# A float32 decoder layer on one core: weight tiles split in one pass, rings of three, one more Strassen pair in each mixer unit

## The chip, the core and the metric

The kernel runs on one core of a Trainium2 chip. The metric is the device time of one execution in microseconds (us). Its engines work in parallel, each on its own queue in order: TensorE (PE) multiplies, VectorE (DVE) and ScalarE (ACT) work elementwise, GpSimd (POOL) and SyncE (SP) here mostly issue DMAs. PE writes to PSUM, which has eight banks of 512 float32 columns; everything else lies in SBUF.

## What is computed

One layer of a decoder over 256 rows of 4096 values. In the reference:

```python
u = rmsnorm(h, norm_w[l])
proj = u @ w_in[l]
a_q, a_f, a_i, a_g, b_q, b_k, b_v, b_g, gate_a, gate_b = jnp.split(proj, split_idx, axis=-1)
o_a = hgrn2_mix(a_q, a_f, a_i, lb_all[l]).astype(u.dtype)
o_a = rmsnorm(o_a, hgrn_norm_w[l]).reshape(bsz, seq, A_WIDTH) * jax.nn.silu(a_g)
...
o_b = diff_attention(qb, kb, vb, lam, slopes)
o_b = rmsnorm(o_b, subln_w[l], SUBLN_EPS) * (1.0 - lam_init)
o_b = o_b.reshape(bsz, seq, B_WIDTH) * jax.nn.silu(b_g)
y = (jax.nn.sigmoid(gate_a) * (o_a @ w_branch_a[l])
     + jax.nn.sigmoid(gate_b) * (o_b @ w_branch_b[l]))
h = h + y @ w_out[l]
return rmsnorm(h, final_w)
```

Nearly all of the work is the four matrix products with w_in (4096 by 24576), the two branch weights (2048 by 4096 each) and w_out (4096 by 4096), all float32.

## The kernel before

**Precision.** A product of float32 values is made of three matmuls in the faster fp32r type: the activations and the weights are each split into a high part (a rounded copy) and a low part (the rest), and high x high, high x low and low x high are added up in PSUM. The activations' parts are made once and stay in SBUF; the weights are streamed from HBM and split on the way: ACT copies the high part (L162), DVE subtracts to get the low part (L163).

**Units and pairs.** The work is a list of units of 1024 output columns: 16 mixer units (m0 to m15: four groups of the HGRN2 recurrence and four of attention, two units each), gate units 0 to 7, four times a branch-A and a branch-B unit, four output units. A unit runs over the contraction in pairs of 128-row tiles: 16 pairs, in a branch unit 8. Each pair's weights are one DMA of 1 MB into a raw tile of 2048 columns (four blocks of 512), of which there are three (`wraw`); SP issues the load when an earlier raw tile has been read out.

**Plain and Strassen pairs.** A plain pair ("P") is 2 tiles x 4 blocks (2 row tiles by 2 column halves) x 3 matmuls = 24 matmuls. A Strassen pair ("S") treats the 2 by 2 blocks of activations and weights in the Winograd variant of Strassen's scheme: 7 products instead of 8, so 21 matmuls, into seven banks. It needs sums of activation blocks, made once for a pair (`s_form`, L375 to L386, one `sf` tile), and sums of weight blocks, made for each raw tile on DVE: L143 adds two blocks in place, L144 makes a third sum in a tile `wt` of its own, L148 subtracts that from two blocks in place. At the end of a unit the seven banks are combined by DVE and ACT (`evict`, L304 to L321). Which pairs are S is listed: SPLIT (L438) for the mixer units from the fourth on and gate units 0 and 1, SPLIT_G (L439) for gate units 2 to 6, SPLIT_B (L468) for branch units, Y_SPLIT for the output units.

**The stream.** `Stream` cuts a pair's weights into chunks: two of 1024 columns for P, four for S (1024, 1024, 512 from `wt`, 1024). Chunks take turns in rings of tiles `hi` and `lo` (1024 columns): 5 of each up to the end of gate unit 0, 7 after it. A ring's tile is free again when PE has read it. `split_to` writes the splitting of a chunk into the program SPLIT_AHEAD (3, later 5) chunks before the matmuls that use it.

**Order.** A scheduler puts each engine's instructions in order when the program is built: of those that are ready in its own estimate, that of the highest priority. The splitting and the combining of banks get a higher priority (`high_priority`, L155 and L290); the matmuls of one bank stay in their order, those of different banks may change places.

**Work between.** The mixers' own steps (transposes, scores, softmax, the heads' norm and gating in `finish`, L690 to L727) are put into a queue and written out one or two after each pair (`step`); those that use PE go only beside pairs 14, 15, 0, 1 and 2, where the four banks of the Strassen products are unused.

Of the kernel before, what the change touches and what calls it, by code (L numbers as in the profile page):

```python
# [37 lines left out]
SPLIT_AHEAD = 3  # L38
# [5 lines left out]
def trunk_kernel(ctx, tc, xT, x, nw, w_mix, w_gate, w_branch, w_out, lbt, hnw, lamv, slw, fw, out):  # L44
# [48 lines left out]
    class Stream:  # L93
# [3 lines left out]

        def __init__(self):
            self.src = []
            self.kind = []  # L100
            self.chunks = []
            self.first = []
            self.raw = {}
            self.split = {}
            self.loaded = 0
            self.done = 0
            self.ring = [(whi, wlo)]
            self.at = 0
# [23 lines left out]
        def tiles(self):  # L132
            a, b = self.ring[self.at % len(self.ring)]
            self.at += 1
            hi = a.tile([P, HALF], F32R, name="hi", tag="hi")
            lo = b.tile([P, HALF], F32R, name="lo", tag="lo")
            return hi, lo

        def sums(self, i, c):
            w = self.raw[i]  # L140
            if c == 0:
                t = self.raw[i, "T"] = wt.tile([P, 512], F32, name="wt", tag="wt")
                dve.tensor_tensor(w[:, 0:512], w[:, 0:512], w[:, 512:1024], op=ALU.add)  # L143
                dve.tensor_tensor(t, w[:, 0:512], w[:, 1536:2048], op=ALU.subtract)  # L144
            if c == 2:
                t = self.raw[i, "T"]
                b = w[:, 512:1536].rearrange("p (a c) -> p a c", a=2)
                dve.tensor_tensor(b, b, t.unsqueeze(1).to_broadcast([P, 2, 512]), op=ALU.subtract)  # L148

        def split_to(self, n):  # L150
            while self.done < min(n, len(self.chunks)):
                i, c = self.chunks[self.done]
                self.load_to(i + 1)
                hi, lo = self.tiles()
                with tc.high_priority(AHEAD):  # L155
                    if self.kind[i] == "S":
                        self.sums(i, c)
                    t = self.raw[i, "T"] if c == 2 else self.raw[i][:, (0, 1024, 0, 512)[c] :]
                    w = 512 if c == 2 else HALF
                    m = HALF // 2 if i < HEAD // 2 else w  # L160
                    for k in range(0, w, m):
                        act.activation(hi[:, k : k + m], t[:, k : k + m], AF.Copy)  # L162
                        dve.tensor_tensor(lo[:, k : k + m], t[:, k : k + m], f32(hi[:, k : k + m]), op=ALU.subtract)  # L163
                if c == (3 if self.kind[i] == "S" else 1):
                    del self.raw[i]
                    self.raw.pop((i, "T"), None)
# [3 lines left out]
        def take(self, i):  # L170
            for n in range(self.first[i], self.first[i] + (4 if self.kind[i] == "S" else 2)):
# [91 lines left out]
    ORDER = (("p5", "P1"), (0, 1), ("P6",), ("P7", 2))  # L263
# [4 lines left out]
    def wide_unit(srcs, kinds, pf, sf, bank, final, post=None, tail=1, kt0=0, pre=None):  # L268
# [55 lines left out]
        def plain(n, c, hi, lo, blocks):  # L324
            kt = kt0 + 2 * n + c
            for t, m in blocks:
                o = 512 * (m if c else 1 - m)
# [3 lines left out]
        def fn(n, c, hi, lo):  # L331
            if pre and c == 0:
                pre(n)
            if kinds[n] == "S":
                for i, b in enumerate(ORDER[c]):
# [9 lines left out]
            if n <= last - tail:  # L345
                plain(n, c, hi, lo, [(t, m if c else 1 - m) for t in range(2) for m in range(2)])
                return
            held[n, c] = hi, lo
            if n < last or c == 0:
                return  # L350
            for blocks in ([[(t, 1 - m)] for t in range(2) for m in range(2)] if tail == 1
                           else [[(t, m) for m in range(2)] for t in range(2)]):
                for (k, c2), w in held.items():
                    plain(k, c2, *w, blocks)
# [83 lines left out]
    SPLIT = (4, 6, 8, 10, 12, 13)  # L438
    SPLIT_G = (0, 2, 4, 6, 8, 10, 12, 13, 14)  # L439
    us = {}  # L440
    s_pools = [sp] * 6
# [19 lines left out]
    def more_sums(n):  # L461
        if n == 0:
            s_pools[:] = [sp2] * 3
# [56 lines left out]
    def branch_unit(q):  # L520
# [46 lines left out]
        def post_b(n):  # L567
            if n == 0:
                g_load(1)
            if q == 3:  # L570
                if n == 0:
                    s_pools[:] = [sp] * 6 + [sp2]
# [102 lines left out]
    with tc.tile_pool(name="tmp", bufs=1) as tmp:  # L675
# [8 lines left out]
        def half(tag):  # L684
            return tmp.tile([P, HPG, P], F32, name=tag, tag=tag)

# [3 lines left out]
        def finish(T, seg, eps, scale, slot):  # L690

            n = 1024 // seg
            o, sq, g = T["o"], T["sq"], T["g"]

            def stats():
                ss = tmp.tile([P, n], F32, name="ss", tag="ss", bufs=2)
                dve.tensor_reduce(ss, fl(sq).rearrange("p (n c) -> p n c", c=seg), axis=AX.X, op=ALU.add)
                act.activation(ss, ss, AF.Sqrt, scale=1.0 / seg, bias=eps)
                dve.reciprocal(ss, ss)
                T["ss"] = ss  # L700

            def gate():
                sg = big("z")
# [4 lines left out]
            def apply():  # L708
                o3 = fl(o).rearrange("p (n c) -> p n c", c=seg)
                dve.tensor_tensor(o3, o3, T["ss"].unsqueeze(2).to_broadcast([P, n, seg]), op=ALU.mult)  # L710
                dve.tensor_tensor(fl(o), fl(o), fl(T["silu"]), op=ALU.mult)
# [65 lines left out]
        def hgrn_group(g):  # L777
# [43 lines left out]
            def s1d():  # L821
                km, kx, dec = T["z"], half("kx"), T["dec"]
                dve.tensor_tensor(km, km, T["sg"], op=ALU.mult)
                dve.tensor_tensor(kx, km[:, :, 0:P], dec[:, :, 1].to_broadcast([P, HPG, P]), op=ALU.mult)
                T["kx"] = kx

            def s2():
                qm, qx, dec = T["q"], half("qx"), T["dec"]
# [219 lines left out]
```

## Time and profile before

| | us |
|---|---|
| median of 3 runs | 2788.42 |
| lowest, highest | 2786.64, 2789.74 |
| the profiled execution | 2788.72 |
| its span, first to last instruction | 2786.9 |
| PE busy | 2760.9 |
| DVE busy | 2341.9 |
| ACT busy | 1616.8 |

By PE's weight matmuls the mixer units end at 1421 us, gate unit 1 ends at 1588, gate units 2 to 6 at 2006, the branch units at 2437. A row of a group names line, engine, operation, tiles (out<-in), shape and count, then busy time, the mean ns of one, and the idle time of the engine before them with what ended it. A row of the timeline has start and length in us first; instructions of one kind that follow each other are merged into one row with their count. PE's matmuls overlap: a matmul's length in the trace is more than the distance to the next.

### The profile page before, as it was taken

The numbers are of one execution on the slowest core, as the hardware profiler recorded it, in microseconds if no ns is written. First come the engines' busy times: TensorE is split into PE (matmuls) and PEld (weight loads), VectorE is DVE, ScalarE is ACT, GpSimd is POOL, SyncE is SP. The second block draws the span as 40 slices with busy tenths as digits, with TensorE's granted clock in tenths as the row PEclk, the third lists the DMA queues.
The fourth block names the chain that finished last, engine by engine and source line by source line (L and its number), as shares of the span: only waits on it lengthen the run. The fifth ranks groups of instructions, "written<-read, shape, count | busy, mean of one in ns | idle before, by whom it ended". The sixth has DMA issues, their size and how long they took to land.

```text
span 2786.9 us, 32847 instructions
## 1 busy us (share of the span) xinstructions
PE 2760.9 (99%) x12361; PEld 2274.4 (82%) x12361; DVE 2341.9 (84%) x2689; ACT 1616.8 (58%) x1937; POOL 74.6 (3%) x124
## 2 busy tenths in 40 slices
PE   9999999999999999999999999999999999999998
PEld 7888888888888888888888887778888888888886
DVE  6784888888888888888888899999877878989997
ACT  7664656656555555665556555555655554555554
POOL 0010000000000000000000000000000000010000
PEclk9999999999999999999999999999999999999999
DMA  9555455555555555555556555555675766766665
GB/s 343 188 181 203 180 185 202 198 199 193 188 191 210 190 192 187 198 206 189 191 196 245 201 212 211 222 214 201 241 263 218 250 218 227 259 235 237 248 255 214
DMA packets 96767, 597.76 MB, mean 214 GB/s; under 512 B 11856, under 2 KB 12128, under 8 KB 31200
## 3 DMA queue, kind: packets, MB, share of 16 engines
q1 hardware_dynamic: 88272, 566.29, 55.9%
q0 software_dynamic: 8336, 29.38, 2.8%
q8 instruction: 96, 1.57, 0.2%
q14 instruction: 63, 0.52, 0.1%
HBM read 571.51 MB, written 24.12 MB: 214 GB/s over the span
## 4 chain that ended last, share of the span: by engine, by line
PE 78%; DVE 14%; DMA 4%; issue 2%; ACT 2%; POOL 0%; DVEq 0%; ACTq 0%; POOLq 0%
PE ps_w L286 75%; DVE lo L163 9%; DVE w L148 2%; DMA w<-in_w_gate 1%; ACT hi L162 1%; DMA w<-in_w_out 1%; DVE w L143 1%; DVE wt L144 1%; PE ps_q L759 1%; DMA w<-in_w_mix 0%; DMA yl<-y_dram 0%; DVE ut L369 0%; PE ps_sc L842 0%; PE ps_o L857 0%; PE ps_t L718 0%
## 5 line engine op out<-in xcount | busy, mean ns | idle before, releaser
L162 ACT ACTIVATE hi<-w 128x1024 fp32r<-128x1024 f32 (+1 forms) x1203 | 1231.5, 1053 | 1009.8 <-PE ps_w L286 497.4
L163 DVE TENSOR_TENSOR lo<-w,hi 128x1024 fp32r<-128x1024 f32 (+1 forms) x1203 | 1436.9, 1219 | 309.0 <-ACT hi L162 291.8
L286 PE MATMUL ps_w<-hi,u 128*128 128x512 f32 x4794 | 1538.8, 391 | 2.0 <-ACT hi L162 2.0
L286 PEld LDWEIGHTS ps_w<-hi,u 128*128 128x128 f32 x4794 | 900.6, 188 | 189.9 <-ACT hi L162 3.4
L286 PE MATMUL ps_w<-lo,u 128*128 128x512 f32 x2397 | 935.5, 390 | 0.9 <-DVE lo L163 0.9
L286 PEld LDWEIGHTS ps_w<-lo,u 128*128 128x128 f32 x2397 | 450.5, 188 | 99.0 <-DVE lo L163 7.1
L286 PE MATMUL ps_w<-hi,sf 128*128 128x512 f32 x1400 | 490.0, 390 | 0.8 <-ACT hi L162 0.7
L286 PEld LDWEIGHTS ps_w<-hi,sf 128*128 128x128 f32 x1400 | 262.8, 188 | 56.9 <-ACT hi L162 1.6
L286 PE MATMUL ps_w<-lo,sf 128*128 128x512 f32 x700 | 274.1, 392 | 8.1 <-DVE lo L163 7.9
L286 PE MATMUL ps_w<-hi,oh 128*128 128x512 f32 x864 | 272.4, 390 | 0.0
L286 PE MATMUL ps_w<-hi,y 128*128 128x512 f32 x784 | 250.1, 390 | 0.0
L148 DVE TENSOR_TENSOR w<-w,wt 128x1024 f32<-128x1024 f32 x175 | 213.6, 1220 | 0.3
L286 PEld LDWEIGHTS ps_w<-hi,oh 128*128 128x128 f32 x864 | 162.2, 188 | 34.3 <-DVE ut L531 1.0
L286 PEld LDWEIGHTS ps_w<-hi,y 128*128 128x128 f32 x784 | 147.2, 188 | 30.7 <-DVE ut L623 0.3
L286 PE MATMUL ps_w<-lo,oh 128*128 128x512 f32 x432 | 168.4, 390 | 0.0
L286 PEld LDWEIGHTS ps_w<-lo,sf 128*128 128x128 f32 x700 | 131.3, 188 | 41.5 <-DVE lo L163 14.7
L143 DVE TENSOR_TENSOR w<-w 128x512 f32<-128x512 f32 x175 | 120.5, 690 | 48.5 <-DMA w<-in_w_mix 27.0
L286 PE MATMUL ps_w<-lo,y 128*128 128x512 f32 x392 | 152.6, 389 | 0.0
L162 ACT ACTIVATE hi<-wt 128x512 fp32r<-128x512 f32 x175 | 109.8, 628 | 48.0 <-PE ps_w L286 32.1
L144 DVE TENSOR_TENSOR wt<-w 128x512 f32<-128x512 f32 x175 | 120.6, 689 | 2.8
L163 DVE TENSOR_TENSOR lo<-wt,hi 128x512 fp32r<-128x512 f32 x175 | 120.1, 686 | 1.8 <-ACT hi L162 1.8
L286 PEld LDWEIGHTS ps_w<-lo,oh 128*128 128x128 f32 x432 | 81.1, 188 | 16.6
(206 smaller groups left out, 1106.5 us busy)
## 6 DMA issues: line engine op xcount, KB each, us to landing
w<-in_w_mix SPq DMA_DIRECT2D x252, 1024.0 KB, 4.8
w<-in_w_gate SPq DMA_DIRECT2D x128, 1024.0 KB, 4.8
w<-in_w_branch SPq DMA_DIRECT2D x64, 1024.0 KB, 4.8
w<-in_w_out SPq DMA_DIRECT2D x64, 1024.0 KB, 5.3
gl<-g_dram SPq DMA_DIRECT2D x32, 256.0 KB, 3.7
g_dram<-ut POOLq DMA_DIRECT2D x28, 256.0 KB, 5.4
o_dram<-s POOLq DMA_DIRECT2D x8, 512.0 KB, 5.9
ol<-o_dram SPq DMA_DIRECT2D x16, 256.0 KB, 4.2
```

Of the source, the lines that this page charges most:

```text
L143: dve.tensor_tensor(w[:, 0:512], w[:, 0:512], w[:, 512:1024], op=ALU.add)
L144: dve.tensor_tensor(t, w[:, 0:512], w[:, 1536:2048], op=ALU.subtract)
L148: dve.tensor_tensor(b, b, t.unsqueeze(1).to_broadcast([P, 2, 512]), op=ALU.subtract)
L162: act.activation(hi[:, k : k + m], t[:, k : k + m], AF.Copy)
L163: dve.tensor_tensor(lo[:, k : k + m], t[:, k : k + m], f32(hi[:, k : k + m]), op=ALU.subtract)
L286: pe.matmul(ps[b], a, w, start=first, stop=left[b] == 0)
L759: pe.transpose(ps[:, j], r[:, j * P : (j + 1) * P], ident)
```

## The change

A chunk becomes up to 2048 columns: one for a plain pair, two for a Strassen pair (blocks 0, 1, 2, 3 as they are after the first sum, then the three others). The rings are three `hi` and three `lo` tiles of 2048 columns throughout; the tiles `wt`, `whi2` and `wlo2` go. The high part of a chunk is made in two ACT passes, the low part of a plain pair and of a Strassen pair's first chunk in one DVE pass of 2048 columns, that of the second chunk in passes of 512 and 1024. The third weight sum is made in place, in a block that the first chunk has read. `begin` writes the sums and high part of the next pair's first chunk ahead of the low part of the current chunk. SPLIT becomes (4, 6, 7, 9, 10, 12, 13), SPLIT_G (2, 4, 6, 7, 9, 10, 12, 13, 14), and the pool `sp` has 7 tiles. The heads' steps use fewer scratch tiles (`z`, `q`, `s1` and `s2` are reused), their sums of squares come from ACT's accumulating Square instead of a DVE reduction, and norm and gate are applied in one DVE pass for each head.

```diff
-SPLIT_AHEAD = 3
+SPLIT_AHEAD = 2
...
-    whi = ctx.enter_context(tc.tile_pool(name="whi", bufs=5))
-    wlo = ctx.enter_context(tc.tile_pool(name="wlo", bufs=5))
-    wt = ctx.enter_context(tc.tile_pool(name="wt", bufs=1))
-    sp = ctx.enter_context(tc.tile_pool(name="sp", bufs=6))
+    whi = ctx.enter_context(tc.tile_pool(name="whi", bufs=3))
+    wlo = ctx.enter_context(tc.tile_pool(name="wlo", bufs=3))
+    sp = ctx.enter_context(tc.tile_pool(name="sp", bufs=7))
...
-            self.chunks.extend((i, c) for c in range(4 if kind == "S" else 2))
+            self.chunks.extend((i, c) for c in range(2 if kind == "S" else 1))
...
+        def tile(self, k):
+            return (whi, wlo)[k].tile([P, PIECE], F32R, name=("hi", "lo")[k], tag=("hi", "lo")[k])
+
+        def sums(self, i):
             w = self.raw[i]
...
+            t2 = w[:, 1536:2048]
+            dve.tensor_tensor(t2, w[:, 0:512], t2, op=ALU.subtract)
+            b = w[:, 512:1536].rearrange("p (a c) -> p a c", a=2)
+            dve.tensor_tensor(b, b, t2.unsqueeze(1).to_broadcast([P, 2, 512]), op=ALU.subtract)
+
+        def begin(self, n):
+            while self.begun < min(n, len(self.chunks)):
+                i, c = self.chunks[self.begun]
+                self.load_to(i + 1)
+                w = self.raw[i]
+                with tc.high_priority(AHEAD):
+                    if c == 1:
+                        self.sums(i)
+                    elif self.kind[i] == "S":
+                        dve.tensor_tensor(w[:, 0:512], w[:, 0:512], w[:, 512:1024], op=ALU.add)
+                    hi = self.tile(0)
+                    cuts = (0, 512, 1024, 1536, 2048) if i < 2 else ((1024, 1536), (0, 1024)) if c else ((1024, 2048), (0, 1024))
+                    for a, b in zip(cuts, cuts[1:]) if i < 2 else cuts:
+                        act.activation(hi[:, a:b], w[:, c * 512 + a : c * 512 + b], AF.Copy)
+                self.hi[self.begun] = hi
+                self.begun += 1
 
         def split_to(self, n):
             while self.done < min(n, len(self.chunks)):
                 i, c = self.chunks[self.done]
...
+                self.begin(self.done + 1)
+                if self.done + 1 < len(self.chunks) and self.chunks[self.done + 1][1] == 0:
+                    self.begin(self.done + 2)
+                w, hi = self.raw[i], self.hi.pop(self.done)
+                lo = self.tile(1)
                 with tc.high_priority(AHEAD):
...
+                    cuts = (0, 512, 1024, 1536, 2048) if i < 2 else ((1024, 1536), (0, 1024)) if c else ((0, 2048),)
+                    for a, b in zip(cuts, cuts[1:]) if i < 2 else cuts:
+                        dve.tensor_tensor(lo[:, a:b], w[:, c * 512 + a : c * 512 + b], f32(hi[:, a:b]), op=ALU.subtract)
...
-    ORDER = (("p5", "P1"), (0, 1), ("P6",), ("P7", 2))
+    ORDER = (((0, 2), (1, 3), ("p5", 0), ("P1", 1)), (("P6", 2), ("P7", 0), (2, 1)))
...
-    SPLIT = (4, 6, 8, 10, 12, 13)
-    SPLIT_G = (0, 2, 4, 6, 8, 10, 12, 13, 14)
+    SPLIT = (4, 6, 7, 9, 10, 12, 13)
+    SPLIT_G = (2, 4, 6, 7, 9, 10, 12, 13, 14)
...
             def apply():
-                o3 = fl(o).rearrange("p (n c) -> p n c", c=seg)
-                dve.tensor_tensor(o3, o3, T["ss"].unsqueeze(2).to_broadcast([P, n, seg]), op=ALU.mult)
-                dve.tensor_tensor(fl(o), fl(o), fl(T["silu"]), op=ALU.mult)
+                for i in range(n):
+                    c = slice(i * seg, (i + 1) * seg)
+                    dve.scalar_tensor_tensor(fl(o)[:, c], fl(o)[:, c], ss[:, i : i + 1], fl(T["silu"])[:, c],
+                                             op0=ALU.mult, op1=ALU.mult)
...
                     pf = ps.rearrange("p h c -> p (h c)")
-                    act.activation(rows(T["o"])[:, tb], pf, AF.Copy)
-                    act.activation(rows(T["sq"])[:, tb], pf, AF.Square)
+                    o = rows(T["o"])[:, tb]
+                    for h in range(HPG):
+                        i = tb * HPG + h
+                        act.activation(o[:, h * P : (h + 1) * P], ps[:, h], AF.Square, accum_out=T["ss"][:, i : i + 1])
+                    act.activation(o, pf, AF.Copy)
...
-    whi2 = ctx.enter_context(tc.tile_pool(name="whi2", bufs=2))
-    wlo2 = ctx.enter_context(tc.tile_pool(name="wlo2", bufs=2))
     sp2 = ctx.enter_context(tc.tile_pool(name="sp2", bufs=3))
     op = ctx.enter_context(tc.tile_pool(name="op", bufs=2))
-    stream.ring = [(whi, wlo)] * 5 + [(whi2, wlo2)] * 2
-    stream.at = 0
-    stream.ahead = 5
```

More of the change, by code (lines that the diff above doesn't have):

```diff
@@ L170, in take @@
         def take(self, i):
-            for n in range(self.first[i], self.first[i] + (4 if self.kind[i] == "S" else 2)):
+            for n in range(self.first[i], self.first[i] + (2 if self.kind[i] == "S" else 1)):
                 self.split_to(n + self.ahead)
@@ L345, in fn @@
             if n <= last - tail:
-                plain(n, c, hi, lo, [(t, m if c else 1 - m) for t in range(2) for m in range(2)])
+                for k in range(2):
+                    plain(n, k, hi, lo, [(t, m if k else 1 - m) for t in range(2) for m in range(2)])
                 return
-            held[n, c] = hi, lo
-            if n < last or c == 0:
+            held[n] = hi, lo
+            if n < last:
                 return
@@ L352, in fn @@
                            else [[(t, m) for m in range(2)] for t in range(2)]):
-                for (k, c2), w in held.items():
-                    plain(k, c2, *w, blocks)
+                for n, w in held.items():
+                    for k in range(2):
+                        plain(n, k, *w, blocks)
         add(srcs, fn, kinds, post)
@@ L961, in f @@
                     pe.matmul(ps[:, 1], aT[:, S : S + P], v[:, 1, c], start=False, stop=True)
[L962 to L963 removed]
+                    o = rows(T["o"])[:, :, c]
+                    for t in range(2):
+                        i = 2 * t + hh
+                        act.activation(o[:, t], ps[:, t], AF.Square, accum_out=T["ss"][:, i : i + 1])
+                    act.activation(o, ps, AF.Copy)
                 return f
```

95 lines of the change are left out of this document (32 added, 63 removed).

## The prediction, made before the change was run

> **What bounds the kernel now.** I read the page's busy times first, then the groups of instructions by shape (count, busy time, mean ns of one, idle time before them), then the chain and the timeline.
>
> ```profile
> span 2786.9 us, 32847 instructions
> PE 2760.9 (99%) x12361; PEld 2274.4 (82%) x12361; DVE 2341.9 (84%) x2689; ACT 1616.8 (58%) x1937; POOL 74.6 (3%) x124
> ...
> L163 DVE TENSOR_TENSOR lo<-w,hi 128x1024 fp32r<-128x1024 f32 x1195 | 1431.8, 1223 | 308.6 <-ACT hi L162 291.4
> L162 ACT ACTIVATE hi<-w 128x1024 fp32r<-128x1024 f32 x1195 | 1226.9, 1056 | 1008.8 <-PE ps_w L286 497.4 <-DVE w L148 341.5 <-DVE w L143 68.2
> ...
> L148 DVE TENSOR_TENSOR w<-w,wt 128x1024 f32<-128x1024 f32 x175 | 213.6, 1220 | 0.3
> L144 DVE TENSOR_TENSOR wt<-w 128x512 f32<-128x512 f32 x175 | 120.6, 689 | 2.8
> L143 DVE TENSOR_TENSOR w<-w 128x512 f32<-128x512 f32 x175 | 120.5, 690 | 48.5 <-DMA w<-in_w_mix 27.0 <-DMA w<-in_w_gate 13.7 <-DMA w<-in_w_out 4.0
> L163 DVE TENSOR_TENSOR lo<-wt,hi 128x512 fp32r<-128x512 f32 x175 | 120.1, 686 | 1.8 <-ACT hi L162 1.8
> L162 ACT ACTIVATE hi<-wt 128x512 fp32r<-128x512 f32 x175 | 109.8, 628 | 48.0 <-PE ps_w L286 32.1 <-DVE wt L144 12.1 <-issue 1.7
> ```
>
> TensorE (PE) is busy throughout and VectorE (DVE) is not far behind. The pace of the weight matmuls is a piece of the chain in which nothing interrupts them; the cost of queued passes is a run of five in the timeline.
>
> ```profile
> 1500.53 72.79 PE ps_w L286 x321
> ...
> 1704.63 4.86 ACT L162 ACTIVATE hi<-w 128x1024 fp32r<-128x1024 f32 x5 [2.78 <-DVE w L148]
> ...
> 1705.76 5.76 DVE L163 TENSOR_TENSOR lo<-w,hi 128x1024 fp32r<-128x1024 f32 x5
> ```
>
> 72.79 us for 321 matmuls is 0.2268 us each. A plain pair of contraction tiles (24 matmuls) thus takes PE 5.44 us, a Strassen pair (21) takes 4.76. A lone 1024-column pass takes DVE 1.22 us, but five in a row take 5.76, so four of them start (5.76 - 1.22)/4 = 1.135 us apart: a queued pass overlaps its forerunner by 0.085. ACT likewise: (4.86 - 1.056)/4 = 0.951. A queued 512-column pass on DVE is then 0.69 - 0.085 = 0.604. The first of ACT's five ends at 1704.63 + 1.056 = 1705.69 and DVE starts at 1705.76: a hand-off between engines is 0.07.
>
> The gate stage with nine Strassen pairs a unit (gate units 2 to 6) is where PE loses most, and the waits say to whom (total, times, longest):
>
> ```profile
> 1588.00:2006.00 418.00, 411.18 (x1789) 333.17 (x1788) 391.12 (x424) 245.41 (x280) 10.30 (x20) 1.00 0.57 213
> ...
> ACT hi L162 <- PE ps_w L286: 529.5, 469, 4.8
> ACT hi L162 <- DVE w L148: 341.5, 137, 5.2
> DVE lo L163 <- ACT hi L162: 293.6, 301, 4.4
> PEld ps_w L286 <- DVE lo L163: 21.8, 34, 1.8
> PE ps_w L286 <- DVE lo L163: 8.7, 13, 1.4
> ```
>
> 1789 matmuls x 0.2268 = 405.7 of 418 us: 12.3 us lost in five units. Elsewhere PE waits for DVE hardly at all, because the split tiles lie ready: ACT waits for PE to free them (the first wait), which is a full ring and costs nothing.
>
> One more thing matters: what PE does when a low part is late. This is mixer unit 3, where two Strassen pairs (12, 13) already stand side by side, as pair 14 begins:
>
> ```profile
> 353.07 2.35 DVE L163 TENSOR_TENSOR lo<-w,hi 128x1024 fp32r<-128x1024 f32 x2
> ...
> 353.33 1.07 PE L286 MATMUL ps_w<-hi,u 128*128 128x512 f32 x4
> 354.34 0.19 PEld L286 LDWEIGHTS ps_w<-lo,u 128*128 128x128 f32 x1 [0.37 <-DVE lo L163]
> ```
>
> Four high-part matmuls run in a row (the last of one block, then three firsts of the next blocks) until the low part lands, and only 0.37 us of idle is left. The order of the instructions is part of the program: each PSUM bank takes its high part first, so up to four matmuls (0.91 us) can go ahead of a late low part.
>
> **Removed from PE.** The 175 passes of L148 count the Strassen pairs. SPLIT grows from six to seven in 15 units (mixer units 3 to 15, gate units 0 and 1); SPLIT_G keeps nine, branch and output units keep theirs. 15 pairs x 3 matmuls x 0.2268 = 10.2 us less on PE.
>
> **The split passes.** No 2048-column pass is in the trace. From below it costs 4 x 0.53 = 2.13 (the slope 1.223 - 0.686 = 0.537 per 512 columns, rounded down, with no fixed part), from above two passes, 2.45. I take the line through the two sizes that are there, 1.223 + 2 x 0.537 = 2.30 alone and 2.21 queued. A plain pair then falls from 2 x 1.135 = 2.27 to 2.21; a Strassen pair from 3 x 0.604 + 4 x 1.135 = 6.35 to 3 x 0.604 + 2 x 1.135 + 2.21 = 6.29. So the merging saves 0.06 us a pair, not the 0.15 that the lone durations suggest; that is nothing on the path by itself. The Trainium skill, page "VectorE: DVE Perf Modes", section "The DRAIN you can't avoid", says that the next op does not start until the pipeline of the one before is empty; the run of five shows starts 0.085 us before the end, so the measurement decides (what the rule would give is a rival below).
>
> **The lead.** This is the step that costs. The rings go from 5 chunks of 1024 (7 after the mixers) to 3 of 2048: PE works on one tile, at most two lie ready, and a tile is freed only when PE has done all of it: 24 matmuls of a plain pair, or the 12 and then 9 of a Strassen pair's two chunks. And 6-7, 9-10, 12-13 now stand side by side, each followed by a plain pair. In such a period (two Strassen, one plain) DVE needs 2 x 6.29 + 2.21 = 14.79 us and PE 2 x 4.76 + 5.44 = 14.96: DVE may idle 0.17 us. It must idle longer. Take the moment at which PE has freed plain pair 5's tile and starts 6, both of whose chunks are ready (chunks written 6a, 6b):
> ACT makes the high part of 7a from 0 to 0.951 + 1.056 = 2.01; DVE, which has no other tile to fill, stands still and then makes its low part, 2.01 to 4.31. The sums of 7b write the raw columns that 7a reads, so they wait for it: the 512 one to 4.91, the 1024 one to 6.05. ACT has the 1024 high part of 7b from 6.05 to 7.10, DVE its low part to 8.3 (the 512 one went in between). ACT's two passes for pair 8 queue behind: to 9.0. DVE's one pass for 8: 9.0 to 11.3, and with four hand-offs of 0.07, 11.6.
> PE is through 6a at 2.72, 6b at 4.76, 7a at 7.48, 7b at 9.52, and with four matmuls ahead wants the low part of 8 at 10.43. It is late by 11.6 - 10.43 = 1.15; I take 1.1 us for a period. From below it is 0: without any wait for ACT, DVE alone would be done at 2.01 + 2.21 + 2 x 0.604 + 2 x 1.135 + 2.30 = 10.0. From above it is 11.6 - 9.52 = 2.05, if no matmul goes ahead. 15 units x 3 periods x 1.1 = 49.5 us.
> The wait is new on DVE, and behind it in DVE's queue stand the sums and all later low parts. Whether one pass or two matters here too: two passes for 8 would have the first half ready at 9.0 + 1.22 + 0.28 = 10.5, and PE starts with that half.
> The Trainium skill, page "Perfetto Trace Analysis", section "Optimizing Scalar/DVE Operations", says that where these engines aren't saturated but cause bubbles elsewhere, breaking instructions up may get work done sooner. That speaks against merging; by it a period kept in halves would cost about 0.1 us. No run here shows it yet.
>
> **The gate units.** Units 2 to 6 go from mostly alternating pairs to 2, 4, 6-7, 9-10, 12-13-14.
>
> ```profile
> L319 DVE TENSOR_TENSOR ut<-ut 128x512 f32<-128x512 f32 x32 | 22.0, 688 | 0.0
> ```
>
> DVE's demand falls a little: 9 x 6.29 + 7 x 2.21 + 8 combining passes x 0.604 = 76.9 us for a unit, against 9 x 4.76 + 7 x 5.44 = 80.9 on PE. But two periods cost 2 x 1.1 and the row of three a period and one Strassen pair more, 1.1 + (6.29 - 4.76) = 2.6. 4.8 x 5 = 24.0, where 12.3 are lost now: 11.7 us more. From both sides: 0 after (12.3 less) and, at 2.05 a period, 7.7 x 5 = 38.5 (26.2 more).
>
> **The rest comes out at nothing.**
>
> ```profile
> L697 DVE TENSOR_REDUCE ss<-s 128x8 f32<-128x1024 f32 x4 | 4.9, 1219 | 1.9 <-ACT s L862 1.9
> L710 DVE TENSOR_TENSOR s<-s,ss 128x1024 f32<-128x1024 f32 x8 | 9.8, 1222 | 0.1
> L711 DVE TENSOR_TENSOR s<-s,z 128x1024 f32<-128x1024 f32 x8 | 9.8, 1219 | 0.0
> L861 ACT ACTIVATE s<-ps_o 128x512 f32<-128x512 f32 x8 | 4.7, 592 | 2.2 <-PE ps_o L859 2.2
> L862 ACT ACTIVATE s<-ps_o 128x512 f32<-128x512 f32 x8 | 4.7, 588 | 0.0
> L927 DVE SCALAR_TENSOR_TENSOR ee<-ps_s,bias 128x128 f32<-128x128 f32 x16 | 4.1, 282 | 3.8 <-PE ps_s L923 3.7
> L382 DVE TENSOR_TENSOR s<-f,s 128x128 f32<-128x128 f32 x9 | 2.9, 324 | 0.1
> L396 DVE TENSOR_TENSOR f<-u 128x512 f32<-128x512 f32 x25 | 17.0, 689 | 0.2
> L385 DVE TENSOR_TENSOR sf<-s,sf 128x512 fp32r<-128x512 f32 x20 | 13.7, 687 | 1.6 <-ACT sf L384 1.6
> w<-in_w_mix SPq DMA_DIRECT2D x252, 1024.0 KB, 4.8
> ```
>
> The heads' end loses a reduction (1.22 us) and two passes (2.44) for eight passes of 128 (8 x 0.28 = 2.3) or four of 256, some 1 us a group off DVE; on ACT the one Square of 0.59 becomes four of 128 columns, of which none is in the trace (between 0.59 in all and 4 x 0.59, 1.8 us more), while PE is busy with plain pairs 0 to 3. If that cover is gone it costs 8 groups x 2 x 1.8 = 29 us at most; ACT at 58% makes me take 0. Shared scratch tiles add waits only among these steps, on ACT and DVE in the units' first pairs; behind them nothing of the split waits long, as it has the higher priority. The seventh transformed tile adds 0.69 + 4 x 0.32 + 0.69 = 2.7 us to DVE in mixer unit 2, which is all plain: hidden, 2.7 if not. Loads take 4.8 us from issue to landing and are issued when a raw tile is read out; pair 9's tile is asked for when 6b is split, at about 0, and wanted at 9: hidden. Output units alternate, 6.29 + 2.21 = 8.5 on DVE against 10.2 on PE: 0.
>
> **Sum.** The profiled execution took 2788.72 us (span 2786.9), 0.3 above the median of 2788.42. 2788.7 - 10.2 + 49.5 + 11.7 = 2839.7.
>
> **The rivals.** *The lead suffices* (not slower): DVE and ACT interleave so that a period is late by less than four matmuls. For it: DVE alone would be done at 10.0, and the 0.37 us in unit 3 shows how much PE can hide; the mixers' transposes give slack too. Against: the wait for ACT at each freed tile is in the data flow. It gives 2788.7 - 10.2 = 2778.5, and 2772 if half of the gates' 12.3 goes as well. It decides below 0.2 us a period (45 x 0.2 = 9, about what PE saves).
> *The order does not help* (much slower): PE takes each block's three in turn, 2.05 a period: 2788.7 - 10.2 + 45 x 2.05 + 26.2 = 2897. For it: orders are fixed at build, and the gates' 12.3 us arose although the same hoisting was open there.
> *No overlap of DVE's passes* (the DRAIN rule as a mechanism here): 13 passes a period x 0.085 = 1.1 more, 2.2 a period: 2788.7 - 10.2 + 45 x 2.2 + 28 = 2906. The five passes in 5.76 us speak against it.
> *The long pass gains nothing*, so that the merge doesn't do what it says: at 2.45 each, three long passes of a period add 0.45, 1.55 in all: 20 us more, 2860, inside my case.
>
> **How the numbers follow.** Forecast 0.55 (its own range 2810 to 2870, prices of 0.6 to 1.6 a period), lead suffices 0.25, order does not help 0.17, no overlap 0.03. 0.2% (5.6 us) is about what a measurement of this kernel can tell from no change. Of the 0.25, 0.20 lies over 0.2% below and 0.05 is hidden only in part, within 0.2%. Slower: 0.55 + 0.17 + 0.03 = 0.75. For 8 in 10 the range reaches from 2776, which leaves out 0.08 of the good case, to 2892, which leaves out 0.1 of the two worst.
>
> **What would show it.** Right: DVE's low-part groups as one 2048 shape at about 2.30 us; weight matmuls 45 fewer (11718); in each mixer unit three places, in pairs 8, 11 and 14, where PE's loads wait for DVE's low part, and a higher total of that wait than 21.8 + 8.7 us; DVE's wait for ACT in repeats of about 2 us after PE frees a plain tile. Wrong: mixer units shorter by 0.7 us each with PE dense, or PE's new idle time at raw loads, at PSUM evictions, or at the heads' steps.

## The result, and the profile after

The changed kernel takes 2899.76 us (median of 4 runs, 2898.41 to 2906.11), the kernel before 2787.79 beside it: a ratio of 1.0405, with a 95% interval of 1.0392 to 1.0418. It is slower by 112 us, where 51 were forecast, and lies above the range (2776 to 2892).

The page of the changed kernel begins with these lines; under them stand its split passes, from the groups with their shapes kept apart.

```profile
span 2898.1 us, 31999 instructions
PE 2813.2 (97%) x12316; PEld 2252.2 (78%) x12316; DVE 2367.8 (82%) x2278; ACT 1614.3 (56%) x2047; POOL 80.6 (3%) x124
...
L171 DVE TENSOR_TENSOR lo<-w,hi 128x2048 fp32r<-128x2048 f32 x510 | 1167.1, 2290 | 338.6 <-ACT hi L156 335.3 <-PE ps_sc L846 0.9 <-PE ps_t L722 0.9
L141 DVE TENSOR_TENSOR w<-w 128x1024 f32<-128x1024 f32 x190 | 232.6, 1224 | 5.8
L139 DVE TENSOR_TENSOR w<-w 128x512 f32<-128x512 f32 x190 | 131.1, 690 | 4.7
L152 DVE TENSOR_TENSOR w<-w 128x512 f32<-128x512 f32 x190 | 130.3, 686 | 55.2 <-DMA w<-in_w_mix 30.0 <-DMA w<-in_w_gate 17.4 <-DMA w<-in_w_out 7.6
L156 ACT ACTIVATE hi<-w 128x512 fp32r<-128x512 f32 x198 | 125.0, 633 | 621.7 <-DVE w L139 581.5 <-PE ps_w L293 26.6 <-issue 8.0
```

PE has the 45 matmuls fewer (12316 against 12361) and yet a span that is 111.2 us longer. The long pass takes 2.290 us, as the line through the shorter ones said (2.30). DVE is busy for 25.9 us more in all, 82% of the span: no engine took PE's place as the busiest. What changed is who waits (total, times, longest):

```profile
ACT hi L156 <- DVE w L139: 581.5, 170, 7.8
DVE lo L171 <- ACT hi L156: 365.2, 337, 5.3
PEld ps_w L293 <- DVE lo L171: 111.8, 133, 3.0
PEld ps_w L293 <- ACT hi L156: 59.1, 140, 1.2
PE ps_w L293 <- DVE lo L171: 57.4, 100, 2.5
```

PE's own waits for the low parts were 21.8 and 8.7 us, and are 111.8 and 57.4. At the head stands ACT's wait for L139, the third weight sum: 581.5 us, or 3.1 us for each of the 190 Strassen pairs. Before, ACT waited little for this sum (12.1 us for L144), but 341.5 us for the 1024 sum behind it (L148). A wait of ACT is not by itself a loss; PE's waits are. The next rows are the two neighbouring pairs 6 and 7 of mixer unit 4, DVE's queue first and then ACT's, from the timeline.

```profile
412.35 2.29 DVE L171 TENSOR_TENSOR lo<-w,hi 128x2048 fp32r<-128x2048 f32 x1
414.67 0.69 DVE L139 TENSOR_TENSOR w<-w 128x512 f32<-128x512 f32 x1
415.40 1.23 DVE L141 TENSOR_TENSOR w<-w 128x1024 f32<-128x1024 f32 x1
416.54 0.68 DVE L171 TENSOR_TENSOR lo<-w,hi 128x512 fp32r<-128x512 f32 x1
417.75 1.23 DVE L171 TENSOR_TENSOR lo<-w,hi 128x1024 fp32r<-128x1024 f32 x1 [0.53 <-ACT hi L156]
419.79 2.29 DVE L171 TENSOR_TENSOR lo<-w,hi 128x2048 fp32r<-128x2048 f32 x1 [0.81 <-ACT hi L156]
422.11 0.69 DVE L139 TENSOR_TENSOR w<-w 128x512 f32<-128x512 f32 x1
...
425.48 2.29 DVE L171 TENSOR_TENSOR lo<-w,hi 128x2048 fp32r<-128x2048 f32 x1 [0.21 <-ACT hi L156]
...
427.69 1.22 DVE L171 TENSOR_TENSOR lo<-w,hi 128x1024 fp32r<-128x1024 f32 x1
...
415.48 0.64 ACT L156 ACTIVATE hi<-w 128x512 fp32r<-128x512 f32 x1 [3.20 <-DVE w L139]
416.65 3.10 ACT L156 ACTIVATE hi<-w 128x1024 fp32r<-128x1024 f32 x3 [0.54 <-DVE w L141]
422.92 5.37 ACT L156 ACTIVATE hi<-w 128x512 fp32r<-128x512 f32 x6 [3.16 <-DVE w L139]
```

These are the links of the prediction's schedule: long low part (412.35), 512 sum, 1024 sum, then ACT's high parts, and DVE standing for them, while ACT has stood for 3.20 us before its 512 pass. Three things differ. DVE stands 0.53 and 0.81 us, where the prediction had it stand 2.01 us before the long low part of pair 7 (here at 419.79). The sums do not overlap with the pass before them: the first begins 0.03 us after its end (412.35 + 2.29 = 414.64, then 414.67), as it overwrites a block that this pass reads; the 512 low part at 416.54, which doesn't depend on the pass before it, starts 0.09 us before that pass ends. And at 425.48 DVE makes pair 8's long low part, and only at 427.69 the last low part of pair 7; the prediction had them the other way round. So both are late together. PE's side of it:

```profile
425.66 0.62 PE L293 MATMUL ps_w<-hi,u 128*128 128x512 f32 x2
426.45 0.50 PE L293 MATMUL ps_w<-hi,sf 128*128 128x512 f32 x1 [0.16 <-ACT hi L156]
426.78 0.63 PE L293 MATMUL ps_w<-hi,u 128*128 128x512 f32 x2
427.82 0.50 PE L293 MATMUL ps_w<-lo,u 128*128 128x512 f32 x1 [0.41 <-DVE lo L171]
```

From 425.90, the start of the second of the first row, to 428.16, where the next matmul starts after the last row, PE starts 5 matmuls in 2.26 us that would take 5 x 0.2268 = 1.13: 1.1 us lost, the price that was forecast. The rows hold five high-part matmuls in a row ahead of the late low part, so it isn't the rival in which the order doesn't help, though that one's 2897 is nearest to the result.

Where the 112 us come from is best seen by stage. Lost time here is the time from a unit's first weight matmul to the next unit's, less its matmuls at 0.2268 us; it holds the mixers' own transposes and scores, too. All columns are profiled executions; the last five are experiments, told below.

| lost us | before | changed | own_tile | s_halves | halves | old_lists | old_rings |
|---|---|---|---|---|---|---|---|
| m0 to m2 | 12.3 | 20.4 | 19.5 | 20.1 | 18.5 | 14.8 | 19.4 |
| m3, m5, m7 | 14.2 | 39.5 | 28.5 | 21.4 | 20.9 | 18.7 | 19.1 |
| m4, m6, m8 | 11.5 | 21.6 | 14.7 | 13.8 | 12.9 | 14.3 | 12.2 |
| m9 to m15 | 36.2 | 61.0 | 47.3 | 43.8 | 39.3 | 44.2 | 40.1 |
| gate unit 0 | 1.3 | 5.0 | 3.0 | 2.4 | 1.8 | 2.6 | 1.5 |
| gate unit 1 | 0.0 | 8.9 | 7.3 | 1.4 | 3.3 | 5.2 | 0.0 |
| gate units 2 to 6 | 12.8 | 40.1 | 30.6 | 20.6 | 15.7 | 39.5 | 9.6 |
| gate unit 7, branches | 6.4 | 5.8 | 5.3 | 6.4 | 6.3 | 6.8 | 7.1 |
| output units | 4.7 | 19.7 | 14.9 | 15.2 | 13.7 | 19.6 | 7.4 |
| all weight matmuls | 2667.8 | 2657.6 | 2657.6 | 2657.6 | 2657.6 | 2667.8 | 2657.6 |

### The profile page after: what moved, and what is told of

Read it like the earlier page. It is cut to its first block, busy times and chain, and to the rows that moved or that the text cites. A ratio compares the mean times of both kernels' runs of the same rounds, so it can differ in the third digit from the quotient of the medians.

```text
span 2898.1 us, 31999 instructions
## 1 busy us (share of the span) xinstructions
PE 2813.2 (97%) x12316; PEld 2252.2 (78%) x12316; DVE 2367.8 (82%) x2278; ACT 1614.3 (56%) x2047; POOL 80.6 (3%) x124
## 4 chain that ended last, share of the span: by engine, by line
PE 75%; DVE 12%; DMA 5%; ACT 5%; issue 2%; POOL 0%; SPq 0%; ACTq 0%; DVEq 0%; POOLq 0%
PE ps_w L293 73%; DVE lo L171 9%; ACT hi L156 4%; DMA w<-in_w_gate 2%; DMA w<-in_w_out 1%; DMA yl<-y_dram 1%; DMA xr<-in_x 1%; DVE w L139 1%; DVE w L152 0%; DMA w<-in_w_mix 0%; PE ps_q L763 0%; POOL s L849 0%; PE ps_s L929 0%; DVE w L141 0%; DMA v<-in_xT 0%
## 5 line engine op out<-in xcount | busy, mean ns | idle before, releaser
L156 ACT ACTIVATE hi<-w 128x1024 fp32r<-128x1024 f32 (+1 forms) x1408 | 1324.3, 991 | 1124.7 <-DVE w L139 581.5
L171 DVE TENSOR_TENSOR lo<-w,hi 128x1024 fp32r<-128x1024 f32 (+2 forms) x898 | 1524.6, 1710 | 368.5 <-ACT hi L156 365.2
L293 PE MATMUL ps_w<-hi,u 128*128 128x512 f32 x4644 | 1513.2, 393 | 4.6 <-ACT hi L156 4.5
L293 PEld LDWEIGHTS ps_w<-hi,u 128*128 128x128 f32 x4644 | 868.6, 188 | 193.4 <-ACT hi L156 22.7
L293 PE MATMUL ps_w<-hi,sf 128*128 128x512 f32 x1520 | 551.7, 396 | 3.4 <-ACT hi L156 3.4
L293 PEld LDWEIGHTS ps_w<-hi,sf 128*128 128x128 f32 x1520 | 286.0, 188 | 91.8 <-ACT hi L156 35.4
L293 PE MATMUL ps_w<-lo,sf 128*128 128x512 f32 x760 | 299.1, 394 | 5.1 <-DVE lo L171 4.7
L141 DVE TENSOR_TENSOR w<-w 128x1024 f32<-128x1024 f32 x190 | 232.6, 1224 | 5.8
L152 DVE TENSOR_TENSOR w<-w 128x512 f32<-128x512 f32 x190 | 130.3, 686 | 55.2 <-DMA w<-in_w_mix 30.0
L139 DVE TENSOR_TENSOR w<-w 128x512 f32<-128x512 f32 x190 | 131.1, 690 | 4.7
L293 PEld LDWEIGHTS ps_w<-lo,y 128*128 128x128 f32 x392 | 73.8, 188 | 27.8 <-DVE lo L171 13.0
```

The lines of the kernel that those rows point to most:

```text
L139: dve.tensor_tensor(t2, w[:, 0:512], t2, op=ALU.subtract)
L141: dve.tensor_tensor(b, b, t2.unsqueeze(1).to_broadcast([P, 2, 512]), op=ALU.subtract)
L156: act.activation(hi[:, a:b], w[:, c * 512 + a : c * 512 + b], AF.Copy)
L171: dve.tensor_tensor(lo[:, a:b], w[:, c * 512 + a : c * 512 + b], f32(hi[:, a:b]), op=ALU.subtract)
L293: pe.matmul(ps[b], a, w, start=first, stop=left[b] == 0)
```

## The experiments

The theory after the prediction was *lead*: three tiles of 2048 hold too little ready work. Its first rivals were *adjacency* (two Strassen pairs in a row can't be supplied, whatever the ring), *long pass* (PE waits for the end of a pass of which it needs the first half) and *heads* (the new heads' steps). Four kernels tell them apart.

**old_rings**: the changed lists and heads' steps on the stream of before, with seven tiles in `sp` (the lines on pools and lists, against the kernel before; the heads' hunks are left out).

```diff
-    sp = ctx.enter_context(tc.tile_pool(name="sp", bufs=6))
+    sp = ctx.enter_context(tc.tile_pool(name="sp", bufs=7))
...
-    SPLIT = (4, 6, 8, 10, 12, 13)
-    SPLIT_G = (0, 2, 4, 6, 8, 10, 12, 13, 14)
+    SPLIT = (4, 6, 7, 9, 10, 12, 13)
+    SPLIT_G = (2, 4, 6, 7, 9, 10, 12, 13, 14)
...
-    sp2 = ctx.enter_context(tc.tile_pool(name="sp2", bufs=3))
+    sp2 = ctx.enter_context(tc.tile_pool(name="sp2", bufs=2))
```

> The kernel before with its rings and passes (5 and 7 chunks of 1024 columns, third sum in its own tile) but with the changed lists of Strassen pairs, the seven tiles in sp, and the changed heads' steps; sp2 has 2 tiles instead of 3 so that it fits. Theory lead (the ring of three holds too little ready work): the same neighbouring Strassen pairs cost almost nothing here, PE's 10.2 us come through, 2775 to 2790 us. Rival adjacency (DVE and ACT can't supply two Strassen pairs in a row, whatever the ring): the three places in each mixer unit lose about 1.1 us each here too, 2820 us or more.

Measured: 2793.82 us, 1.0014 (1.0005 to 1.0023) of before. 106 us of the 112 are gone with the old stream, so adjacency, which had 2820 or more, is not it; the time is 4 us above what lead had. The run doesn't say which part of the stream does it: more tiles, shorter passes and the early third sum come back together. And the 10.2 us that PE saves are used up too: the loss in m0 to m2 is 7.1 us higher than before, in m3, m5 and m7 4.9, in m9 to m15 3.9.

**old_lists**: the changed kernel with the lists of before.

```diff
-    SPLIT = (4, 6, 7, 9, 10, 12, 13)
-    SPLIT_G = (2, 4, 6, 7, 9, 10, 12, 13, 14)
+    SPLIT = (4, 6, 8, 10, 12, 13)
+    SPLIT_G = (0, 2, 4, 6, 8, 10, 12, 13, 14)
```

> The changed kernel with the lists of before (six pairs, mostly alternating). Theory adjacency: nearly all of the loss goes, 2790 to 2810 us. Theory lead: a good part stays, because every extra piece of DVE work (gate units, unit ends, output units) still finds only two tiles ready, 2820 to 2870 us.

Measured: 2855.66 us, 1.0240 (1.0225 to 1.0256). More than half of the loss stays without the seventh pair and its neighbours, as lead had it; adjacency falls again. In gate units 2 to 6 (39.5) and the output units (19.6) all of the loss stays.

**halves**: the changed kernel, every long low part in two passes.

```diff
-                    cuts = (0, 512, 1024, 1536, 2048) if i < 2 else ((1024, 1536), (0, 1024)) if c else ((0, 2048),)
+                    cuts = (0, 512, 1024, 1536, 2048) if i < 2 else ((1024, 1536), (0, 1024)) if c else ((1024, 2048), (0, 1024))
```

> The changed kernel with every 2048-column low part made in two passes of 1024 columns, in the order of ACT's two. Theory long pass (PE waits for the end of a pass of which it needs the first half): the price of a period falls from 1.1 to about 0.1 us, 2830 to 2855 us. Theory lead: the tile is freed and filled at the same times, so within 10 us of the changed kernel, 2890 to 2910 us.

Measured: 2810.12 us, 1.0082 (1.0061 to 1.0102): 90 us of the 112, by undoing the merge alone. The theory of the lead expected no more than 10 and falls; long pass is confirmed, and stronger than it was priced. PE's waits for the low parts show it. ACT's wait for the third sum falls only from 581.5 to 438.5 us, so it is not by itself what costs. From the waits of this kernel:

```profile
ACT hi L156 <- DVE w L139: 438.5, 165, 4.1
PEld ps_w L293 <- DVE lo L171: 44.4, 86, 2.2
PE ps_w L293 <- DVE lo L171: 14.1, 19, 1.8
```

The rule that the prediction set against the merge, of the Trainium skill's page "Perfetto Trace Analysis", section "Optimizing Scalar/DVE Operations" (unsaturated engines that cause bubbles elsewhere: breaking instructions up may help), is borne out here by 90 us.

**heads_only**: the kernel before with the changed heads' steps alone (the hunks from `finish` to attention's `pv`).

> The kernel before with nothing but the changed heads' steps (norm, gate, squares, shared scratch tiles). Forecast and theory lead: no cost, 2782 to 2793 us. Rival heads (the shared scratch and the accumulating squares hold PE up): 2800 us or more.

Measured: 2788.36 us, 0.9998 (0.9989 to 1.0007). Heads falls; the prediction's zero for these steps holds.

Which long pass is it, and by what? Six more kernels vary halves and the changed kernel. Two forms of the long pass are to be told apart: the pass ahead of the Strassen pairs' sums, and the plain pairs' own pass, for which PE waits directly.

**p_halves** and **s_halves** keep one of the two long passes: p_halves that of the Strassen pairs' first chunk, s_halves that of plain pairs.

The end of the changed line in p_halves (s_halves has "S" in place of "P"):

```diff
+ ... if c else ((1024, 2048), (0, 1024)) if self.kind[i] == "P" else ((0, 2048),)
```

> The changed kernel with the low part in halves for plain pairs alone; a Strassen pair's first chunk keeps its one pass of 2048. Theory A (the long pass hurts where a plain pair follows two Strassen pairs, as the prediction's schedule has it: pair 8 late): most of the 90 us that the halves gave comes from here, 2815 to 2845 us. Theory B (the long pass hurts in the Strassen pair's own chain, where the sums of its second chunk stand behind it): 2860 to 2890 us.

> The low part in halves for the Strassen pairs' first chunk alone, plain pairs keep one pass of 2048: the counterpart of p_halves (2861 us). If the two kinds add up: the halves' 2810 plus the 39 us that p_halves gained on the changed kernel, 2842 to 2856 us. If one late place hides the other: below 2840 us.

Measured: p_halves 2861.31 us, 1.0262 (1.0246 to 1.0277); s_halves 2820.15 us, 1.0112 (1.0095 to 1.0129). Halving the Strassen pairs' pass alone gains 80 us on the changed kernel, halving the plain pairs' 38, both 90. So it is mostly the Strassen pairs' first chunk (theory B), and the two gains don't add up to that of both: one late place hides the other.

**own_tile**: the changed kernel, long passes kept, the third sum made early in a tile of its own (the lines of the second chunk that read this tile are left out).

```diff
-            t2 = w[:, 1536:2048]
-            dve.tensor_tensor(t2, w[:, 0:512], t2, op=ALU.subtract)
+            t2 = self.raw[i, "T"]
...
+                        t = self.raw[i, "T"] = wt.tile([P, 512], F32, name="wt", tag="wt")
+                        dve.tensor_tensor(t, w[:, 0:512], w[:, 1536:2048], op=ALU.subtract)
```

> The changed kernel, long passes and all, but with the third weight sum in a tile of its own, made early with the first. Theory in-place sum (the sums stand behind the long pass, and ACT behind the sums): 2850 to 2880 us. Rival long pass alone (the second chunk's 1024 sum and low parts come behind the long pass in DVE's queue anyway): within 8 us of the changed kernel, 2892 to 2908 us.

Measured: 2846.53 us, 1.0210 (1.0195 to 1.0225): 53 us of the loss, so the rival falls, and the gain is larger than the theory had. ACT's largest wait for DVE is now that for the 1024 sum, 279.6 us; in the changed kernel that for the third sum was 581.5:

```profile
ACT hi L159 <- DVE w L141: 279.6, 104, 7.5
PEld ps_w L297 <- DVE lo L175: 67.9, 100, 2.1
PE ps_w L297 <- DVE lo L175: 30.4, 48, 1.7
```

**halves_own**: both edits together.

> The halves with the third weight sum in a tile of its own, made early with the first, as in the kernel before. Theory in-place sum (ACT stands 3 us in each Strassen pair for the sum that must wait for the low part of the first chunk): about half of the 20 us that the halves leave over the kernel before goes, 2795 to 2803 us. Rival ring (three tiles are the limit, whatever the order in them): within 5 us of the halves, 2805 to 2815 us.

Measured: 2810.61 us, 1.0080 (1.0063 to 1.0097), nothing beside the halves, as the rival had it. The long pass and the sum in place are one chain: the second chunk's sums stand behind the first chunk's low part. Shorten the link or take the sum out of it; the second does not help when the first is done.

**halves_swapped**: plain pairs take columns 0 to 1023 first, as PE does.

> Both parts in halves, and for plain pairs in the order in which PE uses them: columns 0 to 1023 first. Theory early start (PE wants the first half of a late tile and could begin a pass sooner): below the halves, 2795 to 2806 us. Theory pipelining (what the halves gave is that DVE begins behind ACT's first pass instead of its second): no change against the halves, 2807 to 2813 us.

Measured: 2805.28 us, 1.0061 (1.0046 to 1.0076), 4.8 below the halves. The expectation had 2795 to 2806 for an early start, so it is there, at the upper end and small: the two intervals overlap, though the slowest of its four runs (2806.82) is below the fastest of the halves (2809.36).

**high_long**: halves, but ACT makes a plain pair's high part in one pass (the end of the line on the high part).

```diff
+ ... if c else ((1024, 2048), (0, 1024)) if self.kind[i] == "S" else ((0, 2048),)
```

> The low part in halves, but the high part of plain pairs in one ACT pass of 2048 columns, so that DVE can begin only when all of the high part is there. Theory pipelining: most of the gain on plain pairs goes, 2840 us or more. Theory shorter last pass (PE's wait ends with the first of the two low passes, wherever they begin): little is lost, 2808 to 2825 us.

Measured: 2825.62 us, 1.0136 (1.0121 to 1.0151), just above the 2825 of the second theory. It gives back 15 us: DVE beginning behind ACT's first pass is worth that much on plain pairs, and most of the halves' gain comes without it.

The last five look for a version that beats both kernels, on the stream of before.

**old_rings_13** (SPLIT_G = 0, 2, 4, 6, 7, 9, 10, 12, 13), **old_rings_8** (SPLIT_G = 2, 4, 6, 7, 9, 10, 12, 13) and **before_8** (the kernel before with SPLIT_G = 0, 2, 4, 6, 8, 10, 12, 13 and nothing else):

> As old_rings (rings and passes of before, seventh pair, new heads' steps), but the gate units' nine pairs are 0, 2, 4, 6, 7, 9, 10, 12, 13, without three in a row. In old_rings gate units 2 to 6 lost 9.6 us. Theory: the row of three is what DVE can't supply there, so about 5 us of it go, 2786 to 2790 us. Rival: DVE's total in a gate unit is the limit, whatever the order, no change, 2791 to 2796 us.

> As old_rings, but the gate units 2 to 6 have eight Strassen pairs (2, 4, 6, 7, 9, 10, 12, 13). PE has 5 x 0.68 = 3.4 us more to do, DVE 5 x 4.1 = 20 us less. Theory DVE's total: the 9.6 us that the gates lose go nearly all, 2786 to 2790 us. Rival neighbours: the pairs side by side keep losing, 2794 to 2798 us.

> The kernel before with eight Strassen pairs in gate units 2 to 6 (pair 14 plain) and nothing else. PE has 3.4 us more, and of the 12.8 us that those units lose most should go: 2778 to 2784 us. Rival: the loss there is at the units' starts and not DVE's total, then 2788 to 2793 us.

Measured: 2795.51 us, 1.0020 (1.0010 to 1.0029); 2783.36 us, 0.9975 (0.9963 to 0.9987); 2779.63 us, 0.9959 (0.9944 to 0.9974). The order of nine pairs doesn't matter (old_rings_13 loses 15.4 us in those units, no less than old_rings), their number does: with eight the gate units lose 1.0 and 1.9 us. In old_rings that was 9.6, before 12.8. That fits DVE's total in a gate unit as the limit there (DVE is busy for 391 of 418 us in the kernel before, ACT for 245); the expectation of old_rings_8 was for 2786 to 2790, and it came out lower still. What is left in before_8 of PE's load waits for the low part (21.8 us before):

```profile
PEld ps_w L286 <- DVE lo L163: 9.7, 22, 1.2
```

**mask_dve**: old_rings_13, with the causal mask of the scores as a product on DVE.

```diff
+                    if tb < 2:
+                        dve.tensor_tensor(sc, ps, tri.unsqueeze(1).to_broadcast([P, HPG, P]), op=ALU.mult)
+                    else:
+                        act.activation(sc, ps, AF.Copy)
```

> As old_rings_13, but the causal mask of the HGRN2 scores is a product on DVE with a triangle, taken straight from PSUM, instead of ACT's copy and GpSimd's select. Theory select (PE stood 4.6 us in mixer unit 1 of old_rings for the first select, and ran at half pace for some us after): 5 to 8 us below old_rings_13. Rival: the wait is for DVE's sums of activations, which stand before the mask on DVE as well, no change within 2 us.

**mask_8**: the same with old_rings_8's list.

> Old rings and passes, seventh pair, eight pairs in gate units 2 to 6 and the mask on DVE. If the gains of old_rings_8 (10 us) and of the mask (9 us) add up: 2772 to 2778 us; if not, 2779 to 2785 us.

Measured: 2786.54 us, 0.9987 (0.9977 to 0.9996), 9.0 below old_rings_13 (5 to 8 were expected), of which 6.8 lie in m0 to m2 (18.5 to 11.7): the select was what PE waited for. mask_8: 2778.77 us, 0.9966 (0.9955 to 0.9978), just between the two ranges; the gains add up only in part. It and before_8 are the fastest, about 10 us below the kernel before, and not to be told apart; before_8 is a change of one list.

## Why the prediction was wrong in its size

- **PE's saving**, 10.2 us: right (45 matmuls fewer). With the old stream, too, it was lost again elsewhere.
- **The long pass**, 2.30 us: right (2.290). Its queued price was not for the sums behind it, which depend on it and don't overlap.
- **The price of a period**, 1.1 us, so 3.3 a unit: right in size in 11 units. m4, m6, m8 to m15 and gate unit 0 lose (21.6 - 11.5) + (61.0 - 36.2) + (5.0 - 1.3) = 38.6 us more than before, 3.5 each. In part that is luck: DVE and ACT take pairs 7 and 8 in another order than in the forecast schedule, and the pass that it would have cut is not the one that matters most (below).
- **The failed step** is that everything outside the forecast schedule was put at that schedule's price or at nothing: 1.1 us for a period in all 15 units, the gate units by periods and one Strassen pair more, and "The rest comes out at nothing". Three terms, the next three points, make the 60 us that were missing.
- **Periods in m3, m5, m7 and gate unit 1** lose 25.3 + 8.9 = 34.2 us more instead of 13.2. The recurrence's steps (m3, m5, m7) and sums of activations (gate unit 1) share DVE there, but this can't be all. In mixer unit 3 the last of these steps on DVE ends at 322.2 us, and pairs 9 to 13, from 339.3 us on, still lose 6.9 us, where those of mixer unit 4 lose 2.8. DVE's order differs: in mixer unit 3 it makes the next Strassen pair's long low part before the last low part of the current one (second row: a pass of 2048 and one of 1024, merged), in mixer unit 4 after it (last two rows). That this order is the reason is argued, not shown.

```profile
340.95 0.69 DVE L171 TENSOR_TENSOR lo<-w,hi 128x512 fp32r<-128x512 f32 x1
342.45 3.43 DVE L171 TENSOR_TENSOR lo<-w,hi 128x2048 fp32r<-128x2048 f32 x2 [0.81 <-ACT hi L156]
...
433.01 0.69 DVE L171 TENSOR_TENSOR lo<-w,hi 128x512 fp32r<-128x512 f32 x1
...
434.22 1.23 DVE L171 TENSOR_TENSOR lo<-w,hi 128x1024 fp32r<-128x1024 f32 x1
436.12 2.29 DVE L171 TENSOR_TENSOR lo<-w,hi 128x2048 fp32r<-128x2048 f32 x1 [0.67 <-ACT hi L156]
```

- **Gate units 2 to 6** lose 27.3 us more instead of 11.7. Counted pair by pair, a unit's two periods cost about 1.6 and 1.3 us and the row of three about 4.2, not 2.6.
- **The rest** is 23.1 us more instead of 0: 15.0 in the output units, 8.1 in m0 to m2. In the output units the sum 6.29 + 2.21 = 8.5 against 10.2 did hold where plain and Strassen pairs alternate: output units 1 and 2 lose 0.4 us together from pair 3 on (the row below is 50 us of output unit 2, in which PE is never idle). Some 14 of the 19.7 us lie in the units' first three pairs, where DVE still combines the banks and adds up the rows of the unit before; the sum did not hold these. Of the 14, about 5 are one wait for a DMA and the slow clock behind it (last section). Another 3.6 lie in pairs 8 and 9 of output unit 0, its first Strassen pair and the plain one behind it. In m0 to m2, 6 of the 8.1 us lie at the end of mixer unit 1. The prediction took the seventh tile's sums as hidden; the last section shows what they held up.

```profile
2730.00:2780.00 50.00, 50.00 (x222) 1.00 0.59 227
```

- **The cause** was in the main put into the wrong part. The text called the lead of three tiles the step that costs, and named the long pass as something that "matters here too", for pair 8's own pass. With the same three tiles halves lose 90 us less, and in the 11 units they lose 0.45 us a unit more than before, no more than old_rings (0.44). Nor is it mainly pair 8's pass: by the same count p_halves, which cut that one, keep 2.4 of the 3.5 us, and s_halves, which cut the Strassen pairs' first chunk, 1.0. The rule against merging was weighed for one place of a period and not for the whole stream. Whether a longer lead would have hidden the long passes too is open: no run has them with more than three tiles.
- **Its sums** hold but for roundings: 4 x 0.53 is 2.12 and not 2.13, 11.6 - 9.52 is 2.08 and not 2.05. Nothing hangs on them.
- **Rivals.** Long pass gains nothing, order does not help, no overlap: none is what happened; of the last it is true that the two sums behind a long pass, which depend on it, don't overlap. "The lead suffices" came closest to the truth for the old rings, and there the sum was still not better than before.
- What is left open: halves_swapped still stands 11.5 us above old_rings, mostly in gate unit 1 (5.6 against 0.0) and the output units (13.1 against 7.4). The stream of before frees tiles of 1024 and after the mixers holds seven; a fourth tile of 2048 for those stages was not tried. So the ring's own share in these stages is argued, not shown.

## What to carry to other kernels

Before merging two instructions, look for who waits for the first half, and for what stands behind it in the same chain: a merge that saves 0.06 us of an engine's time can lengthen a chain of five links by a microsecond each time. A sum of busy times below the bound engine's held for a steady stretch of alternating pairs, and said nothing about the starts of units and the rows of two or three Strassen pairs. And where DVE is near PE's total, one Strassen pair fewer can be faster (before_8), though PE then has more matmuls.

## What the hardware showed beside this

In output unit 3 DVE stood 4.11 us for a row tile from HBM, a low part stood behind it, and PE ran dry. These rows are DVE's and PE's from the timeline of the changed kernel, and then a window of 6 us with the granted clock behind PE's loads:

```profile
2806.30 0.69 DVE L633 TENSOR_TENSOR ut<-ut,xr 128x512 f32<-128x512 f32 x1 [4.11 <-DMA xr<-in_x]
...
2809.85 0.80 PE L293 MATMUL ps_w<-lo,y 128*128 128x512 f32 x1 [2.55 <-DVE lo L171]
...
2809.90:2815.90 6.00, 6.00 (x14) 4.74 (x15) 5.89 (x9) 4.81 (x6) 1.60 (x3) 0.50 0.88 268
```

After 2.55 us without a matmul the clock was 0.50 for the next 6 us: 14 matmuls, 0.43 us apart, cost 14 x 0.43 - 14 x 0.2268 = 2.8 us on top of the wait. The Trainium skill, page "TensorE: Matmul & The Clock Gate", section "What's actually happening", gives an idle window of about 3.4 us for the fall to half the clock; here the shorter idle was enough. In s_halves, too, 3.3 us at a clock of 0.50 (from 2653.00) followed an idle of 1.79; behind the idle times of 1.30 us in gate unit 1 of the changed kernel (1596.71, 1608.85) the clock stayed at 1.00.

PE also stood in mixer unit 1, 5.42 us, and ran at a clock of 0.50 behind it: the first two selects on GpSimd took 11.19 us together, against 7.06 in the kernel before. These rows are GpSimd's, PE's and DVE's from the timeline of the changed kernel.

```profile
183.79 11.19 POOL L849 TENSOR_SCALAR_AFFINE_SELECT s<-s 128x512 f32<-128x512 f32 x2 [169.05 <-ACT s L847]
...
194.45 2.08 PE L862 MATMUL ps_o<-v,s 128*128 128x128 f32 x8 [5.42 <-POOL s L849]
...
191.62 2.28 DVE L171 TENSOR_TENSOR lo<-w,hi 128x2048 fp32r<-128x2048 f32 x1
198.25 0.69 DVE L394 TENSOR_TENSOR sf<-s,sf 128x512 fp32r<-128x512 f32 x1 [4.36 <-ACT sf L393]
```

The eight selects took between 0.63 and 10.6 us each, for one shape. The traces show when the long one ends. While the first select runs, DVE's passes follow each other without a pause until 193.90 (191.62 + 2.28), and the select, 10.61 us long, ends at 194.40, 0.50 us later. In the kernel before DVE's first pause is one of 0.03 us at 188.30, and the select, 6.42 us long, ends at 188.80, again 0.50 us later; so it is in heads_only and old_rings (10.70 us). With six Strassen pairs in SPLIT, so six sums of activations, the first select takes 6.42 (before, heads_only) or 7.00 us (old_lists), with seven 10.34 to 10.70 (changed, old_rings, halves). So the seventh tile's sums, which go into DVE's unbroken row, were not hidden: GpSimd and PE stood for that row. The Trainium skill, page "SBUF — State Buffer", section "Who interferes with whom", has a rule that fits in part: a DVE operation with two inputs from SBUF and a GpSimd operation that reads SBUF shut each other out for a whole instruction, and every split pass of DVE has two such inputs. Here it was not one instruction but the whole row up to DVE's first pause. No run changes DVE's inputs alone, so the port itself is not shown as the cause.
